# Seven chunks for six in a LoRA projection, with a 16-row store placed between the loads

## The chip, the cores and the metric

The kernel runs on one core of a Trainium2 chip. The metric is the device time of one execution in microseconds (us), lower is better.

## The reference

```python
x_flat = x.reshape(-1, in_dim)              # (16*2048, 256) float32
y = x_flat @ W                              # W: 256 x 256
lora_out = x_flat @ lora_A                  # lora_A: 256 x 16
lora_out = lora_out * lora_E                # 16 values
lora_out = lora_out @ lora_B                # lora_B: 16 x 256
y = y + scale * lora_out
return y.reshape(batch, seq_len, out_dim).astype(np.float32)
```

x and y hold 32,768 rows of 256 float32 each, 33.55 MB in and 33.55 MB out.

## The kernel before

The adapter is folded into the weights first: `weff` = W + A · diag(E · scale) · B, in bfloat16 (lines 148 to 167). After that the kernel is one matrix product, y = x · weff.

**Rows and chunks.** In this text a *row* is a row of one partition: 128 partitions hold one each, so a row of a chunk stands for 128 rows of x, 128 KB. The 256 such rows are cut by `PLAN` into chunks of 48, 32, 48, 48, 48 and 32. A partition's share of a chunk lies contiguously in HBM (`rows_of`), so one transfer of 48 rows moves 48 KB for each of the 128 partitions. `PIECES` lets the loads of chunks 0 and 2 be issued in two pieces each (16 and 32 rows, 24 and 24).

**Slots.** Chunks live in SBUF in four buffers, `SLOTS` = 48, 32, 48 and 48 rows, 176 in all. Chunk i uses slot i modulo 4. The result is written over the input: ScalarE copies y from PSUM into the slot that x came from (line 214), and the store goes out from there. Chunks 4 and 5 use the slots of chunks 0 and 1 again.

**The steps.** A chunk is worked through in steps of S = 8 rows, 32 steps in all. For each step VectorE casts x to bfloat16 (`rounded`, line 141), TensorE transposes it into PSUM as eight blocks (`transposed`, L180), VectorE copies the transposed block to SBUF (`copied`, L145), TensorE multiplies it with `weff` (`multiplied`, L191, 16 matmuls), and ScalarE copies the result into the slot in two halves (L214). VectorE runs two steps ahead in the order copied(t), rounded(t + 2). TensorE runs one step ahead: it transposes step t + 1 before it multiplies step t. So the last step of a chunk is multiplied only after the first step of the next chunk has arrived and been cast.

**The queue of transfers.** All loads and stores of x and y are issued by SyncE, in the order of its program. Before the steps start it issues the first piece of chunk 0, W, the rest of chunk 0, and chunks 1 to 3 (lines 113 to 121). After that, for each chunk in turn, it waits until the chunk's last result has been copied (line 223), issues the store, and then, where `AFTER` names later chunks, waits until the store that frees a slot has landed and issues the load (lines 225 to 227). `AFTER = {1: [4, 5]}` puts loads 4 and 5 behind store 1. The transfers are served in this order: loads 0 to 3, stores 0 and 1, loads 4 and 5, stores 2 to 5.

**The hold.** `HOLD = {3: 1}` makes VectorE wait, ahead of the first cast of chunk 3, until store 1 has landed (lines 136 to 140). The data don't ask for this wait. VectorE works in order, so the copy of the last transposed step of chunk 2, which stands behind it, waits as well, and with it that step's product and store 2.

Of the kernel before, what the change touches and what calls it, by code (L numbers as in the profile page):

```python
# [3 lines left out]

PLAN = [48, 32, 48, 48, 48, 32]

PIECES = {0: [16, 32], 2: [24, 24]}

SLOTS = [48, 32, 48, 48]
LEAD = 4  # L10
AFTER = {1: [4, 5]}

HOLD = {3: 1}

S, G = 8, 4
P = 128
# [17 lines left out]
def kernel(tc, x, W, lora_A, lora_B, lora_E, scale, out):  # L34
    nc = tc.nc
# [5 lines left out]
    KC = K // P  # L41
    assert K == M and sum(PLAN) * P == N
    starts = [sum(PLAN[:i]) * P for i in range(len(PLAN))]

    steps = [(i, r) for i, b in enumerate(PLAN) for r in range(0, b, S)]
    NS = len(steps)
    assert NS % 2 == 0

    def rows_of(flat, i):
        b, r0 = PLAN[i], starts[i]  # L50
        return flat[r0:r0 + b * P, :].rearrange("(p b) k -> p b k", b=b)

    def sbuf(name, shape, dt):
        return nc.alloc_sbuf_tensor(name, shape, dt).ap()
# [3 lines left out]

    slots = [sbuf(f"xy{s}", [P, rows, K], FP32) for s, rows in enumerate(SLOTS)]
    a_sb = sbuf("a_sb", [P, KC, R], FP32)  # L60
# [21 lines left out]
    pieces = {}  # L82
    for i, b in enumerate(PLAN):
        parts = PIECES.get(i, [b])
        pieces[i] = [(sum(parts[:j]), n) for j, n in enumerate(parts)]
    s_ld = {(i, r): Count(nc, f"s_ld{i}_{r}") for i in pieces for r, n in pieces[i]}
    s_st = [Count(nc, f"s_st{i}") for i in range(len(PLAN))]
    s_id, s_set, s_v, s_t, s_m, s_y = (
# [5 lines left out]
    can_y = [[nc.alloc_semaphore(f"can_y{h}_{k}") for k in range(2)] for h in range(S // G)]  # L94

    def slot(i):
        return slots[i % LEAD][:, :PLAN[i], :]

    def load(i, parts=None):
        for r, n in parts or pieces[i]:  # L100
            s_ld[i, r].by(nc.sync.dma_start(out=slot(i)[:, r:r + n, :], in_=rows_of(x_flat, i)[:, r:r + n, :]), 16)

    def store(i):
        s_st[i].by(nc.sync.dma_start(out=rows_of(out_flat, i), in_=slot(i)), 16)
# [6 lines left out]


    with tc.tile_critical(no_gpsimd_drain=True):
        load(0, pieces[0][:1])
        s_w.by(nc.sync.dma_start(out=w_sb, in_=W.rearrange("(p c) m -> p c m", c=KC)), 16)
        s_a.by(nc.scalar.dma_start(out=a_sb, in_=lora_A.rearrange("(p c) r -> p c r", c=KC)), 16)
        s_b.by(nc.scalar.dma_start(out=b_sb, in_=lora_B), 16)
        s_e.by(nc.scalar.dma_start(out=e_sb, in_=lora_E[:, None]), 16)
        load(0, pieces[0][1:])
        for i in range(1, LEAD):  # L120
            load(i)
    tc.close()
    tc.compile()  # L123
# [8 lines left out]
    def rounded(t):  # L132
        i, r = steps[t]
        if (i, r) in s_ld:
            nc.vector.wait_ge(s_ld[i, r].sem, 16)
        if i in HOLD and r == 0:

            for _ in range(10):
                nc.vector.engine_nop()
            nc.vector.wait_ge(s_st[HOLD[i]].sem, 16)  # L140
        nc.vector.tensor_copy(out=xb[t % 2], in_=slot(i)[:, r:r + S, :]).then_inc(can_t[t % 2], 1)  # L141
# [68 lines left out]
    for i, r in [(i, r + g) for i, r in steps for g in range(0, S, G)]:  # L210
        n += 1
        nc.scalar.wait_ge(s_m.sem, n)
        t, h = divmod(n - 1, S // G)
        y = nc.scalar.copy(out=slot(i)[:, r:r + G, :], in_=ps_y[h])  # L214
        free = can_y[h][(t + 1) % 2]
        if r + G < PLAN[i]:
            y.then_inc(free, 1)
        else:
            done = s_y.by(y)
            if n < s_m.total:  # L220
                nc.scalar.wait_ge(s_y.sem, done)
                nc.scalar.sem_inc(free, 1)
            nc.sync.wait_ge(s_y.sem, done)
            store(i)
            for later in AFTER.get(i, []):
                nc.sync.wait_ge(s_st[later - LEAD].sem, 16)
                load(later)


# [44 lines left out]
```

## Time and profile before

| what | value |
|---|---|
| median of 3 runs | 162.41 us (162.36 to 163.22) |
| the profiled execution | 162.57 us |
| its span, first to last recorded instruction | 161.3 us |
| read from HBM, written | 33.85 MB, 33.55 MB |
| mean rate of DMA over the span | 418 GB/s |
| mean granted clock of TensorE | 0.82 |

The profile divides the span into 40 slices and gives, for each engine, the busy share in tenths:

```profile
PE   0149179999999980000009999999999970000000
PEld 0038058999999960000008899999999960000000
DVE  0074197898989800000039589898989500000000
ACT  0300406777768680000000577776868680000000
...
PEclk9999978999999998555555899999999997555555
```

The compute engines work in two blocks, from about 20 to 60 us and from about 84 to 133 us. TensorE's granted clock falls to 0.5 where it stands idle and is back to full some 8 us into a block. The groups by cost show what one instruction of each kind takes (busy time, mean ns, idle time before):

```profile
L214 ACT COPY xy<-psum_y 128x1024 f32<-128x1024 f32 x64 | 61.9, 1015 | 64.0 <-PE psum_y L191 64.0
L191 PE MATMUL psum_y<-weff,xt 128*128 128x256 bf16 x512 | 64.9, 283 | 0.1
L141 DVE CAST xb<-xy 128x2048 bf16<-128x2048 f32 x32 | 39.0, 1217 | 32.3 <-DMA out_dram<-xy 26.8
L145 DVE COPY xt<-psum_xt 128x1024 f32<-128x1024 f32 x32 | 39.2, 1224 | 11.2 <-PE psum_xt L180 11.2
```

The cast's 26.8 us of waiting for a store is the hold.

### The profile page before, as it was taken

To read this page: it belongs to the slowest core of one execution; us is meant where nothing else is said; L and a number is where in the kernel's file an instruction comes from. 1 tells how busy PE (TensorE), PEld (TensorE's weight loads), DVE (VectorE), ACT (ScalarE), POOL (GpSimd) and SP (SyncE) were. 2 spreads that over 40 slices of the span, in tenths; PEclk is the share of its full clock that TensorE was granted. 3 is DMA by queue.
4 is the path that set the end of the run, shared out by engine and by line. 5 is a ranking of instruction groups with operands and counts; after the bars stand their busy time and mean duration, and the time that the engine had idled before them with its cause. 6 is when DMAs were issued, how large, how long until landed. Compare 5 with 4: busy or idle time off the path is not lost.

```text
span 161.3 us, 1875 instructions
## 1 busy us (share of the span) xinstructions
PE 93.2 (58%) x780; PEld 83.4 (52%) x780; DVE 76.6 (48%) x67; ACT 63.2 (39%) x65; POOL 0.7 (0%) x6
## 2 busy tenths in 40 slices
PE   0149179999999980000009999999999970000000
PEld 0038058999999960000008899999999960000000
DVE  0074197898989800000039589898989500000000
ACT  0300406777768680000000577776868680000000
POOL 0100000000000000000000000000000000000000
PEclk9999978999999998555555899999999997555555
DMA  4999999999999999989999989999999999999993
GB/s 137 407 496 423 423 423 433 408 463 408 506 439 427 402 390 392 500 386 398 480 435 402 500 378 406 471 431 404 463 463 415 402 451 463 427 402 402 447 447 171
DMA packets 2370, 67.42 MB, mean 418 GB/s; under 512 B 432, under 2 KB 448, under 8 KB 576
## 3 DMA queue, kind: packets, MB, share of 16 engines
q1 hardware_dynamic: 2160, 67.37, 97.7%
q10 hardware_dynamic: 208, 0.03, 0.1%
q14 instruction: 2, 0.02, 0.0%
HBM read 33.85 MB, written 33.55 MB: 418 GB/s over the span
## 4 chain that ended last, share of the span: by engine, by line
PE 44%; DMA 22%; ACT 2%; DVE 1%; issue 0%
PE psum_y L191 29%; DMA out_dram<-xy 22%; PE psum_xt L180 14%; ACT xy L214 2%; DVE xb L141 1%
## 5 line engine op out<-in xcount | busy, mean ns | idle before, releaser
L214 ACT COPY xy<-psum_y 128x1024 f32<-128x1024 f32 x64 | 61.9, 1015 | 64.0 <-PE psum_y L191 64.0
L191 PE MATMUL psum_y<-weff,xt 128*128 128x256 bf16 x512 | 64.9, 283 | 0.1
L191 PEld LDWEIGHTS psum_y<-weff,xt 128*128 128x128 bf16 x512 | 51.8, 101 | 7.6 <-issue 0.3
L141 DVE CAST xb<-xy 128x2048 bf16<-128x2048 f32 x32 | 39.0, 1217 | 32.3 <-DMA out_dram<-xy 26.8
L180 PE MATMUL psum_xt<-ident,xb 128*128 128x128 f32 x264 | 37.1, 288 | 29.7 <-DVE xb L141 29.7
L180 PEld LDWEIGHTS psum_xt<-ident,xb 128*128 128x128 f32 x264 | 32.3, 150 | 31.3 <-DVE xb L141 30.9
L145 DVE COPY xt<-psum_xt 128x1024 f32<-128x1024 f32 x32 | 39.2, 1224 | 11.2 <-PE psum_xt L180 11.2
L153 PE MATMUL psum_xt<-ident,a_sb 128*16 128x128 f32 x2 | 0.6, 397 | 6.8 <-POOL ident L127 6.8
L149 DVE CAST b_bf<-b_sb 16x256 bf16<-16x256 f32 x1 | 0.3, 281 | 7.9 <-DMA b_sb<-in_lora_B_dram 7.9
L214 ACT ACT_TABLE_LOAD x1 | 1.3, 1283 | 6.0 <-PEq L123 6.0
L153 PEld LDWEIGHTS psum_xt<-ident,a_sb 128*16 128x16 f32 x2 | 0.1, 90 | 6.7 <-DMA a_sb<-in_lora_A_dram 6.7
L162 PE MATMUL psum_xt<-b_bf,ate 16*128 16x256 bf16 x2 | 0.6, 402 | 2.4 <-DVE ate L157 2.4
L162 PEld LDWEIGHTS psum_xt<-b_bf,ate 16*128 16x128 bf16 x2 | 0.1, 104 | 2.9 <-DVE ate L157 2.9
L157 DVE TENSOR_SCALAR ate<-psum_xt,e_sb 16x256 bf16<-16x256 f32 x1 | 0.5, 473 | 1.0 <-DMA e_sb<-in_lora_E_dram 1.0
L167 DVE TENSOR_TENSOR weff<-w_sb,psum_xt 128x512 bf16<-128x512 f32 x1 | 0.7, 669 | 0.0
L127 POOL TENSOR_SCALAR_AFFINE_SELECT ident<-ident 128x128 f32<-128x128 f32 x1 | 0.3, 292 | 0.2 <-POOL ident L125 0.2
L125 POOL MEMSET ident<- 128x128 f32 x1 | 0.2, 205 | 5.4 <-POOLq L123 5.4
L255 POOL MEMSET const-bfloat16-1.0<- 128x1 bf16 x1 | 0.1, 102 | 0.0
L255 POOL MEMSET const-uint8-127<- 128x1 uint8 x1 | 0.1, 101 | 0.0
L255 POOL MEMSET const-float32-0.0<- 128x1 f32 x1 | 0.1, 98 | 0.2 <-issue 0.2
L255 POOL MEMSET const-float32-1.0<- 128x1 f32 x1 | 0.1, 98 | 0.0
## 6 DMA issues: line engine op xcount, KB each, us to landing
out_dram<-xy SPq DMA_DIRECT2D x4, 6144.0 KB, 30.6
xy<-in_x_dram SPq DMA_DIRECT2D x3, 4096.0 KB, 24.5
xy<-in_x_dram SPq DMA_DIRECT2D x2, 6144.0 KB, 39.3
out_dram<-xy SPq DMA_DIRECT2D x2, 4096.0 KB, 31.8
xy<-in_x_dram SPq DMA_DIRECT2D x2, 3072.0 KB, 36.7
xy<-in_x_dram SPq DMA_DIRECT2D x1, 2048.0 KB, 8.4
w_sb<-in_W_dram SPq DMA_DIRECT2D x1, 256.0 KB, 8.5
a_sb<-in_lora_A_dram ACTq DMA_DIRECT2D x1, 16.0 KB, 5.7
```

The lines of the kernel that those rows point to most:

```text
L127: s_id.by(nc.gpsimd.affine_select(out=ident, in_=ident, compare_op=mybir.AluOpType.not_equal, fill=1.0, base=0, pattern=[[-1, P]], channel ...
L141: nc.vector.tensor_copy(out=xb[t % 2], in_=slot(i)[:, r:r + S, :]).then_inc(can_t[t % 2], 1)
L145: nc.vector.tensor_copy(out=xt[t % 2], in_=ps_xt[t % 2]).then_inc(can_m, 1)
L149: s_v.by(nc.vector.tensor_copy(out=b_bf, in_=b_sb))
L153: at_done = nc.tensor.transpose(ps_at[:, c, :], a_sb[:, c, :], ident)
L157: s_v.by(nc.vector.tensor_scalar(out=ate, in0=ps_at, scalar1=e_sb, scalar2=float(scale), op0=mybir.AluOpType.mult, op1=mybir.AluOpType.mult))
L162: aeb_done = nc.tensor.matmul(ps_aeb[:, c, :], ate[:, c, :], b_bf, start=True, stop=True)
L167: s_v.by(nc.vector.tensor_add(out=weff, in0=w_sb, in1=ps_aeb))
L180: done = nc.tensor.transpose(ps_xt[k][:, j, :], words[k][:, j, :], ident)
L191: done = nc.tensor.matmul(ps_y[h][:, j, :], pairs[k][:, h * G + j, :, c], weff[:, c, :], start=(c == 0), stop=(c == KC - 1))
L214: y = nc.scalar.copy(out=slot(i)[:, r:r + G, :], in_=ps_y[h])
L255: nc = _bacc.Bacc("TRN2", target_bir_lowering=False, num_devices=1)
```

## The change

`PLAN` becomes seven chunks of 16, 32, 48, 48, 32, 32 and 48 rows, each loaded in one piece. The slots become five, 16, 32, 48, 48 and 32 rows, again 176 in all. A table `HEIR` replaces the modulo: chunk 5 takes the slot of chunk 1, and chunk 6 that of chunk 2; the slots of chunks 0, 3 and 4 are used once. Only `FIRST` = 3 chunks, 96 rows, are loaded before the first store. `AFTER` puts loads 3 and 4 behind store 0, with no wait for any landing, since their slots have not been used, and loads 5 and 6 behind store 2, which wait for the landings of stores 1 and 2. The hold moves to chunk 4, which waits for store 2. The instructions of TensorE, VectorE, ScalarE and GpSimd are the same, in the same order, but for the place of the hold (step 18 in place of 16) and the waits for loads.

The order of the queue before and after (L load, S store, rows in brackets; W is loaded after the first 16 rows in both):

```
before: L0a(16) W L0b(32) L1(32) L2a(24) L2b(24) L3(48) S0(48) S1(32) L4(48) L5(32) S2(48) S3(48) S4(48) S5(32)
after:  L0(16)  W L1(32)  L2(48) S0(16) L3(48) L4(32) S1(32) S2(48) L5(32) L6(48) S3(48) S4(32) S5(32) S6(48)
```

```diff
-PLAN = [48, 32, 48, 48, 48, 32]
-
-PIECES = {0: [16, 32], 2: [24, 24]}
-
-SLOTS = [48, 32, 48, 48]
-LEAD = 4
-AFTER = {1: [4, 5]}
-
-HOLD = {3: 1}
+PLAN = [16, 32, 48, 48, 32, 32, 48]
+
+PIECES = {}
+
+SLOTS = [16, 32, 48, 48, 32]
+LEAD = 5
+HEIR = {5: 1, 6: 2}
+
+FIRST = 3
+AFTER = {0: [3, 4], 2: [5, 6]}
+
+HOLD = {4: 2}
...
     def slot(i):
-        return slots[i % LEAD][:, :PLAN[i], :]
+        return slots[HEIR.get(i, i)][:, :PLAN[i], :]
...
     with tc.tile_critical(no_gpsimd_drain=True):
-        load(0, pieces[0][:1])
+        load(0)
         s_w.by(nc.sync.dma_start(out=w_sb, in_=W.rearrange("(p c) m -> p c m", c=KC)), 16)
...
-        load(0, pieces[0][1:])
-        for i in range(1, LEAD):
+        for i in range(1, FIRST):
             load(i)
...
             for later in AFTER.get(i, []):
-                nc.sync.wait_ge(s_st[later - LEAD].sem, 16)
+                if later in HEIR:
+                    nc.sync.wait_ge(s_st[HEIR[later]].sem, 16)
                 load(later)
```

## The prediction

> **What bounds the kernel now.** I read the page's busy time first, then the row of DMA shares and the queue table, then the SyncE queue's own waits, and last the timeline around each store's issue.
>
> ```profile
> span 161.3 us, 1875 instructions
> PE 93.2 (58%) x780; PEld 83.4 (52%) x780; DVE 76.6 (48%) x67; ACT 63.2 (39%) x65; POOL 0.7 (0%) x6
> DMA  4999999999999999989999989999999999999993
> q1 hardware_dynamic: 2160, 67.37, 97.7%
> PE psum_y L191 29%; DMA out_dram<-xy 22%; PE psum_xt L180 14%; ACT xy L214 2%; DVE xb L141 1%
> ```
>
> No compute engine is busy for more than 58% of the span. The DMA row reads 9 or 8 in every slice but the first and the last, and one queue's packets fill 97.7% of what 16 engines can do in the span. The chain of waits (last line) names PE, but it follows the last store back through what let it be issued; the queue's own order is not in it. So I checked the SyncE queue's waits (us in total, times, longest), the group of all stores, and the timeline at the last store:
>
> ```profile
> SPq L104 <- ACT xy L214: 90.0, 6, 31.4
> SPq L101 <- DMA out_dram<-xy: 35.0, 2, 25.6
> ...
> DMA to landing us min/median/max: 28.0/30.6/36.5
> ...
> 133.27 0.33 SPq L104 DMA_DIRECT2D out_dram<-xy  x1
> ```
>
> A store takes 28.0 us or more from issue to landing, though its 48 rows need only 14.5 us of transfer (below): it stands behind other transfers. The last store is issued at 133.27 and the span ends at 161.3, with the engines full in between. The path is therefore the first load's start, then one unbroken stream of 67.4 MB. I write L0, L1... for loads, S0, S1... for stores. All go through SyncE's queue, and the landings follow the order of issue.
>
> The trace's records of single packets give the price of the stream. Each transfer puts 8 packets on each of the 16 engines. From one packet's start to the next, undisturbed, it is 1.812 us for 48 rows, 1.209 for 32 and 0.606 for 16: a transfer of 48, 32 or 16 rows holds the engines for 14.50, 9.68 or 4.85 us. The first packet starts at 1.99 us, 1.05 after its issue; the last packet ends at 160.3 and lands at 161.24, 0.95 later. Between these, no engine has a gap. What the packets took over 0.611, 0.912, 1.213 and 1.815 us (16, 24, 32, 48 rows) is 1.57 us per engine: 0.65 at the head, 0.53 from 52 to 64, where loads give way to S0, 0.11 from 104 to 112 (L5 to S2), 0.02 where stores give way to L4 at 82, and about 0.013 to 0.016 per 4 us where compute runs beside the transfers.
>
> ```profile
> 48.00:52.00 4.00, 4.00 (x39) 3.71 (x38) 3.74 (x4) 2.95 (x4) 0.00 (x0) 1.00 1.02 442
> 52.00:56.00 4.00, 4.00 (x39) 3.73 (x38) 3.48 (x4) 2.83 (x3) 0.00 (x0) 1.00 1.11 430
> 56.00:60.00 4.00, 3.68 (x34) 3.14 (x32) 0.57 (x1) 3.09 (x4) 0.00 (x0) 1.00 0.92 393
> 80.00:84.00 4.00, 0.00 (x0) 0.00 (x0) 0.62 (x1) 0.00 (x0) 0.00 (x0) 0.50 1.14 492
> ```
>
> The columns are PE, PEld, DVE, ACT, POOL, clock, DMA share and GB/s. A packet counts where it ends, so one slice swings between 0.9 and 1.14; the turn from loads to stores shows as 430 and then 393 GB/s, the turn back (80 to 84) as no loss.
>
> **The change, part by part.** *Bytes and packets.* Before there are 8 loads and 6 stores, after 7 and 7; 256 rows go in and 256 out in both. 14 transfers of 8 packets per engine stay 14, so the stream's nominal length does not change: 0.
>
> *Is the stream kept unbroken?* The queue becomes L0(16) W L1(32) L2(48) S0(16) L3(48) L4(32) S1(32) S2(48) L5(32) L6(48) S3(48) S4(32) S5(32) S6(48). W ends at about 8.6 in the trace, and up to there the order is unchanged (the 16-row piece of L0 is now L0, the 32-row piece is L1). Adding the prices above, transfers end at: L1 18.3, L2 32.8, S0 37.6, L3 52.1, L4 61.8, S1 71.5, S2 86.0, L5 95.7, L6 110.2, S3 124.7, S4 134.3, S5 144.0, S6 158.5. Each issue must come about 1.05 us before its predecessor's end.
>
> The new danger is S0, since SyncE now waits for chunk 0's results with L3 and L4 behind that wait. Chunk 0 is two steps of 8 rows; PE multiplies step 1 only after it has transposed step 2, which lies in L1. Before, step 2 lay in the 32-row second piece of L0, at the same place of the queue, so the old timeline gives the time: the copies of step 1 are
>
> ```profile
> 23.98 1.01 ACT L214 COPY xy<-psum_y 128x1024 f32<-128x1024 f32 x1 [6.21 <-PE psum_y L191]
> 25.65 1.01 ACT L214 COPY xy<-psum_y 128x1024 f32<-128x1024 f32 x1 [0.66 <-PE psum_y L191]
> ```
>
> so S0 is issued at 25.65 + 1.01 = 26.7, L3 and L4 by 27.9 (0.34 to 0.79 each). The queue would run dry at 32.8: slack 32.8 - 26.7 - 1.05 = 5.0 us. Cost 0.
>
> For the others I take a restart after a pause as 7.7 us from the first cast to the store's issue (83.38 to 91.12 before, at the clock's 0.50) and a step as 2.62 (pairs of ACT copies start at 32.64 and 35.26). L2 lands about 33.8; S1 is issued by 33.8 + 7.7 = 41.5 (needed by 60.7). L3 lands at 53.1, S2 by 60.8 (needed 70.4). L5 waits for S1's landing, 72.5 (needed 84.9); L6 for S2's, 87.0 (needed 94.6, slack 7.6). The hold on chunk 4 (DVE waits for S2; behind it the copy of chunk 3's last step, and with that S3) ends at 87.0: S3 at 94.7 (needed 109.1), S4 four steps later at 105.2 (123.6), S5 after L6's landing at 111.2 + 7.7 = 118.9 (133.3), S6 six steps on, 134.6 (142.9). The least slack is 5.0: nothing of compute, holds or waits reaches the path. Chunk 2 as one load instead of two pieces makes PE pause until 33.8; the 19 us of slack at S1 hide it.
>
> *The turns.* Before the stream turns from loads to stores twice and back once; after, three times and twice. This is the only part on the path. The turn back: 0.02 per engine, taken as 0. The turn to stores: 0.11 and 0.53 per engine in the two rows; seen at the landing of the last engine, L5 comes 9.99 after L4 instead of 9.68 (0.31), and L3 with S0 14.95 + 14.84 instead of 14.55 + 14.50 (0.74). The last engine sets the end, so one more turn costs between 0.31 and 0.74. The dearer row has 48-row packets in all 16 engines' last load slowed to 1.9 to 2.6 us; the cheaper one 32-row packets, of which only some are slowed. The three new ones are 48 to 16 rows, 32 to 32 and 48 to 48. The first resembles the dearer row on its load side, the cheaper in its short store, so I take the middle, 0.5, and keep for the range that it gains (-0.3, if the dear price belongs to the first store ever or to its size) and that all three are dear (3 x 0.74 - 1.05 = +1.2).
>
> The Trainium skill speaks against the change here: its page "DMA: Bandwidth & Descriptors", section "Anatomy of one DMA", gives each DMA about 2 us fixed, mostly the write's receipt (a fit for DMAs that GpSimd issues). If each turn paid that openly, two more turns would be an estimated 4 us. In this queue S3 follows S2 by 14.5 us, its bare transfer, and the turn at 82 shows no gap; the trace disagrees where a successor is already queued.
>
> *The head.* L0's packets now come from rows 16 KB apart per partition instead of 48 KB. The excess there is 0.65; it could go (-0.65) or, by the same size, double. Taken as 0.
>
> Sum: 0 + 0 + 0.5 = +0.5 on the profiled 162.57 (span 161.3 and 1.3 around it), 163.1; the median of the runs is 162.41, 0.16 lower, so the forecast is 162.9.
>
> **The rivals.**
> - *The short store smears its turn* (slower). Engines end 1.4 to 2 us apart, and S0 lasts only 4.85, so some read while others write from L2's end into L3. Price: one slowed 48-row packet of +0.5 (2.3 against 1.8) at L2's end and one or two at L3's start, +0.5 again at the later turns: +1.5 in all, 163.9. It decides when L3's first packets are over 2.0 us. For it: every engine was hit at the old first turn. Against: the turn back at 82 cost nothing.
> - *Turns are cheap or the dear one is only the first*: -0.3, 162.1. For: 0.11 at the second turn. Against: both are the same kind of meeting.
> - *Faster*: the closer rows take the head's 0.65 away and the smaller store takes 0.4 of the first turn (0.53 to 0.11): -1.0, 161.4. Against: from 4 us on L0's packets already run at 0.611.
> - *S0 comes late and starves the queue*: were chunk 0's end to wait for L2, S0 would be issued at 41.5, with the queue dry from 32.8: 41.5 + 1.05 - 32.8 = 9.8, so 172. Against: the two copies above.
> - *Each turn drains the queue*: 1.05 before a first packet and 0.95 after a last are 2.0 per turn, two more turns 4.0, 166.4. (The rule of the Trainium skill above says the same.) Against: no gap at any of three turns.
> - That the store does not stand between the loads I give nothing of its own: landings keep the order of issue.
>
> **How the numbers follow.** Forecast 0.52 (its own range 162.3 to 163.4), smeared turns 0.20, cheap turns 0.10, faster 0.10, starved 0.05, drained 0.03. A measurement of this kernel tells about 0.5%, 0.8 us, from no change: under 161.6 is faster, over 163.2 slower. Faster: 0.10 and 0.02 of the cheap case, 0.12. Slower: 0.28 and 0.06 of the forecast's upper edge, 0.34. The rest, 0.54, is no change. The range 161.8 to 164.2 takes in the smeared and the cheap case and leaves out the starved and drained ones and most of the faster one, 0.18.
>
> **What would show it.** Right: S0 issued near 26.7 and landing near 39; DMA shares at 9 throughout; three dips at about 32, 61 and 109 us; every later store issued long before its turn in the queue; span near 161.8. Wrong: a DMA slice of 7 or less between 30 and 45 (starved); packets of L3 over 2.0 us (smeared); a head whose 16-row packets differ from 0.65 us of excess. A queue share under 96% at a longer span would mean that I missed a gap.

## The result and the profile after

The changed kernel takes 162.75 us in the median of 22 runs (162.53 to 163.28), the kernel before 162.46 us (162.23 to 163.22). The ratio is 1.0019, with a 95% interval of 1.0012 to 1.0026: 0.31 us slower by the ratio (0.19 to 0.42 by its interval), which 22 runs of each can tell from nothing, though it is under the 0.5% set as the bound. The forecast was 162.9 and "no change".

The profiled execution took 163.04 us, the third slowest of the 22 and 0.29 over their median. The lines of the page that answer to those of before:

```profile
span 161.7 us, 1876 instructions
PE 95.8 (59%) x780; PEld 84.4 (52%) x780; DVE 76.0 (47%) x67; ACT 63.2 (39%) x65; POOL 0.7 (0%) x6
DMA  3999999989989999999899999999999999999992
q1 hardware_dynamic: 2160, 67.37, 97.0%
PE psum_y L193 7%; PE psum_xt L182 3%; ACT xy L216 1%
```

The DMA row is still 8 or 9 in every slice but the first and last. The chain of waits (last line) now covers some 11% of the span: it is followed back from the last store, which was issued long before its turn, so it says little of the end in either kernel. The queue of SyncE, first its waits, then the group of all stores, then the timeline at store 0:

```profile
SPq L107 <- ACT xy L216: 98.2, 7, 22.6
SPq L104 <- DMA out_dram<-xy: 28.4, 2, 14.2
...
DMA to landing us min/median/max: 13.1/29.1/31.9
...
26.81 0.35 SPq L107 DMA_DIRECT2D out_dram<-xy  x1
```

Store 0 is issued at 26.81 (26.7 was predicted), and no store waits less than 13.1 us from issue to landing.

So the stream is as unbroken as before, and yet the span is longer. Where the time went shows in the landings. Each transfer ends on 16 DMA engines, and the trace has each engine's landing. The spread between the first and the last engine, in us from the span's start:

```
                     last store: first, median, last engine   spread
kernel before              159.25     159.72     161.22         1.97
changed kernel             159.27     159.51     161.69         2.42
```

The first engine ends at the same time in both kernels, and the median engine even 0.21 us earlier in the changed one. Only the last engine is later. The same spread at each landing from load 1 on (us; L load, S store):

```
kernel before   L1 1.07  L2a 1.06  L2b 1.06  L3 1.15  S0 1.46  S1 1.13  L4 1.46  L5 1.74  S2 1.77  S3 1.97  S4 2.00  S5 1.97
changed kernel  L1 1.04  L2 1.58  S0 1.33  L3 1.52  L4 2.24  S1 2.24  S2 2.08  L5 2.25  L6 2.34  S3 2.37  S4 2.40  S5 2.41  S6 2.42
```

In the changed kernel's trace nearly all of it is there when load 4 lands. Load 2 adds 0.54 us and load 4 adds 0.72; they are the last loads ahead of the first and the second turn from loads to stores, and one packet of load 4 ran over by 729 ns. All that follows adds 0.18. But this is one execution. The changed kernel without its hold (below), the same up to there, has 0.63 and 0.98 us at these two landings, after 0.90 at load 1. Four of the experiments below (the work added behind the last step) are the kernel before up to 133 us, and in these and the kernel before the spread at the landing of load 5 is 1.70 to 2.00 us: one trace of each kernel can't settle 0.3 us.

The excess that I had priced as a mean over the engines fell from 1.57 to 0.99 us, while the time rose: the mean doesn't set the end.

Of that mean, the three turns from loads to stores took 0.32, 0.10 and 0.06 us in the changed kernel, 0.48 in all, against 0.53 and 0.11 before. The head took 0.29 instead of 0.65, but that is one execution: with the same first load it was 0.51, 0.77 and 0.60 in three of the experiments.

Looking for what else makes an engine late, I listed the store packets that took longer than their 1.815 us (48 rows). In the kernel before, from 112 to 132 us, start in us and excess in ns:

```
113.7:90 115.6:113 117.5:99 119.4:109 121.4:112 123.3:99 125.2:99 127.1:109 129.0:123 131.0:109
```

The starts are 1.9 us apart, which is one packet and its excess: these are the successive packets of a single engine, while the 15 others have none over 30 ns. They stop at 132 us, when TensorE stops. A trace doesn't name the engine of a packet; that it is one is read from this spacing. I had read the same numbers as "0.013 to 0.016 per 4 us where compute runs beside the transfers", a mean over 16. On the one engine it is 16 times as much, 0.1 us in 1.8.

The changed kernel has such an engine too. When the packets are joined end to start, it ends 1.87 us behind the first engine in both kernels. Before, that made it the last. In the changed kernel's trace another engine ends last, 2.45 us behind, and none of its store packets ran over. So this trace doesn't show the slowed stores as the cause of the later end.

How much TensorE works beside stores is a view of the profile: the windows in which stores hold the queue (columns PE, PEld, DVE, ACT, POOL, clock, DMA share, GB/s; x is the number of instructions). Before, stores 0 and 1, then 2 to 5:

```profile
57.00:82.00 25.00, 2.68 (x25) 2.23 (x23) 0.00 (x0) 3.07 (x4) 0.00 (x0) 0.62 1.02 439
105.50:160.00 54.50, 26.65 (x245) 24.55 (x242) 20.06 (x17) 20.81 (x22) 0.00 (x0) 0.77 0.98 425
```

After, store 0, then 1 and 2, then 3 to 6:

```profile
33.00:38.00 5.00, 2.20 (x14) 1.90 (x12) 2.89 (x3) 1.68 (x2) 0.00 (x0) 0.77 0.99 423
62.00:86.00 24.00, 9.95 (x92) 8.96 (x89) 6.33 (x6) 8.28 (x9) 0.00 (x0) 0.80 1.01 437
110.50:160.00 49.50, 21.35 (x193) 19.16 (x190) 15.11 (x13) 16.52 (x18) 0.00 (x0) 0.78 0.98 425
```

TensorE is busy beside stores for 29.3 us with 270 matmuls (transposes counted in) before, and for 33.5 us with 299 after. The change puts chunk 3's steps beside store 1 (62 to 71 us).

### The profile page after: what moved, and what is told of

Its sections match the earlier page's. It is cut to its first block, busy times and chain, and to the rows that moved or that the text cites. A ratio compares the mean times of both kernels' runs of the same rounds, so it can differ in the third digit from the quotient of the medians.

```text
span 161.7 us, 1876 instructions
## 1 busy us (share of the span) xinstructions
PE 95.8 (59%) x780; PEld 84.4 (52%) x780; DVE 76.0 (47%) x67; ACT 63.2 (39%) x65; POOL 0.7 (0%) x6
## 5 line engine op out<-in xcount | busy, mean ns | idle before, releaser
L182 PE MATMUL psum_xt<-ident,xb 128*128 128x128 f32 x264 | 38.4, 295 | 27.9 <-DVE xb L143 27.9
L182 PEld LDWEIGHTS psum_xt<-ident,xb 128*128 128x128 f32 x264 | 32.9, 152 | 30.4 <-DVE xb L143 30.0
## 6 DMA issues: line engine op xcount, KB each, us to landing
out_dram<-xy SPq DMA_DIRECT2D x1, 2048.0 KB, 13.1
```

Of the source, the lines that this page charges most:

```text
L182: done = nc.tensor.transpose(ps_xt[k][:, j, :], words[k][:, j, :], ident)
```

## The experiments

The first four runs were made to test the third turn against the chunks, the head and the hold; the one-engine theory came out of them. Ratios are to the kernel before, timed beside it on the same chip. The matmul count is the sum of PE's x over the store windows, as above.

**Two turns.** Loads 3 and 4 go ahead of store 0.

```diff
-FIRST = 3
-AFTER = {0: [3, 4], 2: [5, 6]}
+FIRST = 5
+AFTER = {2: [5, 6]}
```

> The change's chunks and slots, but loads 3 and 4 issued before store 0: the stream turns from loads to stores twice, as in the kernel before, not three times. Theory (the third turn costs the 0.3 us): back to 162.4 to 162.5, ratio 0.999 to 1.001. Rival (the new chunks, the contiguous first load or the place of the hold cost it): 162.75, ratio 1.002. A head that got cheaper (0.29 against 0.65 us of excess per engine in the two traces) would show here alone: 162.1 to 162.3.

Measured: 162.5 us, ratio 1.0001 (0.9985 to 1.0017). Matmuls beside stores: 271. The interval just leaves out 1.0019, so chunks, first load and hold by themselves are hardly the cause, and no gain from the head shows. It speaks for the turn, but the matmul count fell as well.

**The turn alone.** In the kernel before, load 3 goes behind store 0.

```diff
-AFTER = {1: [4, 5]}
+FIRST = 3
+AFTER = {0: [3], 1: [4, 5]}
...
-        for i in range(1, LEAD):
+        for i in range(1, FIRST):
...
-                nc.sync.wait_ge(s_st[later - LEAD].sem, 16)
+                if later >= LEAD:
+                    nc.sync.wait_ge(s_st[later - LEAD].sem, 16)
```

> The kernel before with its own chunks, slots, pieces and hold, but load 3 issued behind store 0: three turns from loads to stores, nothing else changed. Theory: 0.3 us slower than before, 162.7 to 163.0, ratio 1.002 to 1.003, and the last engine's lag behind the first grows at the landing of the load ahead of each turn. Rival (chunks, head, hold): unchanged, 162.46, ratio 1.000.

Measured: 163.62 us, ratio 1.0057 (1.0035 to 1.0079). The direction is the theory's, the size two to three times too large for it. Store 0 now goes out while chunks 1 and 2 are computed:

```profile
42.50:57.50 15.00, 15.00 (x140) 13.98 (x139) 12.38 (x11) 11.30 (x12) 0.00 (x0) 1.00 1.03 442
71.50:81.50 10.00, 0.00 (x0) 0.00 (x0) 0.00 (x0) 0.00 (x0) 0.00 (x0) 0.50 0.99 427
105.50:162.00 56.50, 26.53 (x244) 24.43 (x241) 19.93 (x17) 20.69 (x22) 0.00 (x0) 0.75 0.95 410
```

That is 384 matmuls beside stores. From 42.9 to 56.3 us one engine's packets run 90 to 167 ns over, eight in a row, and the last engine ends 4.1 us behind the first. This profiled execution took 164.62 us, 1.0 over the median, so its spread is not the typical one.

**Four turns.** Load 4 moves behind store 1.

```diff
-AFTER = {0: [3, 4], 2: [5, 6]}
+AFTER = {0: [3], 1: [4], 2: [5, 6]}
```

> The changed kernel with load 4 moved behind store 1: four turns from loads to stores. Theory: another 0.3 us (0.1 to 0.7), 163.0 to 163.3, ratio to the kernel before 1.004 (1.002 to 1.007). Rival (a turn is free once the first is paid): 162.75, ratio 1.002.

Measured: 162.89 us, ratio 1.003 (1.0006 to 1.0054); 279 matmuls beside stores. Between the two expectations it is inconclusive: the interval holds both values. Seven of the twelve executions took 162.31 to 162.96 us, five 163.31 to 163.96.

**No hold.** The changed kernel without its hold.

```diff
-HOLD = {4: 2}
+HOLD = {}
```

> The changed kernel without the hold of chunk 4. Theory (compute is nowhere on the path, packets beside compute take 0.3% longer for the same number of steps): 162.75, ratio 1.002. Rival (the hold keeps compute away from a turn, and its new place costs the time): 0.2 us or more away from 162.75, to either side.

Measured: 163.4 us, ratio 1.0059 (1.0036 to 1.0082), 0.65 us over the changed kernel's median with the same three turns. A premise of my theory fell here: compute does reach the path. Whether a turn costs time as well, this run doesn't tell. Without the hold chunk 4 is computed beside stores 1 and 2; with 28 matmuls beside store 0 it is 410 in all:

```profile
62.00:86.50 24.50, 21.49 (x197) 19.74 (x195) 16.55 (x15) 17.04 (x18) 0.00 (x0) 1.00 1.01 434
110.50:160.00 49.50, 20.52 (x185) 18.35 (x182) 15.11 (x13) 15.70 (x17) 0.00 (x0) 0.75 0.98 424
```

**No hold in the kernel before.** The new theory was put to a kernel with two turns.

```diff
-HOLD = {3: 1}
+HOLD = {}
```

> The kernel before without its hold: still two turns from loads to stores, the same queue, the same chunks, but chunk 3 is computed from about 60 us on, beside stores 0 and 1, and TensorE's work beside stores grows from 28 us to about 41. Theory now (one of the 16 DMA engines serves store packets some 5 to 6% slower while the compute engines work, and that engine ends last; the five runs so far give 0.06 us for each us of compute beside stores): 0.6 to 0.9 us slower, ratio 1.0035 to 1.0055, and one engine with packets 0.05 to 0.12 us longer from about 60 to 77 us. Rival (the number of turns sets the time): ratio 1.000.

Measured: 163.56 us, ratio 1.0061 (1.0041 to 1.0081), with 398 matmuls beside stores. Two turns, and as slow as three turns with 410 matmuls. The direction and the size are the theory's, a little above its range (1.0035 to 1.0055). One engine's packets run 80 to 127 ns over from 61.6 to 71.2 us, as it had said. It also tells what the hold does: it keeps chunk 3's compute away from stores 0 and 1.

```profile
57.00:82.00 25.00, 18.73 (x169) 16.72 (x166) 13.88 (x12) 14.60 (x16) 0.00 (x0) 0.96 1.03 443
105.50:160.00 54.50, 24.99 (x229) 22.96 (x227) 18.66 (x16) 19.27 (x20) 0.00 (x0) 0.77 0.98 425
```

**Which engine does it.** Three kernels add work behind the last step, where in the kernel before no packet is over by more than 21 ns. Its results go to PSUM or SBUF that nobody reads; SyncE starts it with a semaphore once the last result is in.

```diff
...
+    for _ in range(12):
+        for j in range(2 * G):
+            for c in range(KC):
+                nc.tensor.matmul(ps_y[j // G][:, j % G, :], pairs[1][:, j, :, c], weff[:, c, :],
+                                 start=(c == 0), stop=(c == KC - 1))
```

> The kernel before, and behind its last step 192 matmuls more on TensorE alone, into PSUM that nobody reads, from about 134 to 155 us, where stores 4 and 5 go out and no packet was over its time in any of the six traces. If TensorE is what slows the one DMA engine: 8 or more packets of stores 4 and 5 some 0.1 us (48 rows) and 0.07 us (32 rows) longer, about 1 us on the last landing, 163.3 to 163.6. If not: no packet over its time by more than 0.03 us after 135 us, 162.4 to 162.7.

```diff
...
+    for _ in range(18):
+        s_q.by(nc.vector.tensor_copy(out=xt[0], in_=ps_xt[1]))
+        nc.vector.wait_ge(s_q.sem, s_q.total)
...
```

> As before it, with 18 PSUM copies of 128 x 1024 on VectorE alone from about 134 to 157 us. If VectorE slows the one DMA engine: packets of stores 4 and 5 longer by 0.05 to 0.12 us on one engine, 163.3 to 163.6. If not: none, 162.4 to 162.7.

```diff
...
+    for _ in range(20):
+        s_q.by(nc.scalar.copy(out=xt[0], in_=ps_xt[1]))
+        nc.scalar.wait_ge(s_q.sem, s_q.total)
...
```

> As before it, with 20 PSUM copies of 128 x 1024 on ScalarE alone from about 134 to 156 us. If ScalarE slows the one DMA engine: packets of stores 4 and 5 longer by 0.05 to 0.12 us on one engine, 163.3 to 163.6. If not: none, 162.4 to 162.7. If none of the three alone does it, it takes them together or their traffic of semaphores.

The packets that ran over by more than 25 ns from 134 us on (start in us, excess in ns):

```
TensorE:  134.6:90 136.5:98 138.4:80 140.0:412 140.3:71 142.1:85 144.0:80 145.9:71 147.8:80 149.7:99 151.6:60 152.9:61 154.0:369 154.2:47
VectorE:  none
ScalarE:  154.3:33
```

TensorE alone does it, packet after packet until its last matmul starts at 154.5 us. One execution each took 163.54 (TensorE), 162.82 (VectorE) and 163.39 us (ScalarE). The last two miss their expectation of 162.4 to 162.7, but with at most one packet over they do so hardly through the added work. In the run of ScalarE the last engine was 2.6 us behind the first already at store 3, most of which went out before that work began.

**Half the instructions.** The same time on TensorE, with 96 matmuls of 512 columns.

```diff
...
+    wide = weff[:, :, :].rearrange("p c m -> p (c m)")
+    for _ in range(12):
+        for j in range(2 * G):
+            nc.tensor.matmul(ps_y[j // G][:, j % G // 2 * 2:j % G // 2 * 2 + 2, :].rearrange("p g m -> p (g m)"),
+                             pairs[1][:, j, :, 0], wide, start=True, stop=True)
```

> As the run with 192 matmuls of 256 columns behind the last step, but 96 of 512 columns: the same time on TensorE with half the instructions. If the slowing goes with TensorE's busy time: packets of store 4 some 0.1 us longer on one DMA engine, as there. If it goes with the number of its instructions: some 0.05 us. Time 163.3 to 163.6 in the first case, 162.8 to 163.2 in the second.

Measured: 162.85 us, and packets over by 32 to 46 ns, but for one of 80 and a single one of 400, which has its like at 140.0 above:

```
134.6:43 136.4:46 138.3:43 139.6:400 140.1:33 142.0:43 143.8:43 145.7:33 147.5:33 149.4:80 151.3:32
```

The windows of the two kernels, first 256 columns, then 512:

```profile
136.00:152.00 16.00, 16.00 (x149) 14.34 (x148) 0.00 (x0) 0.00 (x0) 0.00 (x0) 1.00 0.99 427
```

```profile
136.00:152.00 16.00, 16.00 (x76) 7.23 (x74) 0.00 (x0) 0.00 (x0) 0.00 (x0) 1.00 0.99 428
```

TensorE is busy for all 16 us in both. Some 8.5 packets at 80 ns are 680 ns over 149 matmuls, 4.6 ns for each; some 8.7 at 41 ns are 357 ns over 76, 4.7 ns. The slowing goes with the number of TensorE's instructions, not with its busy time. The weight loads halve along with the matmuls (PEld 14.34 and 7.23 us), so which of the two counts isn't told. These are single executions.

**Finer pieces.** Two kernels lower the count by starting TensorE earlier. In the kernel before:

```diff
-PIECES = {0: [16, 32], 2: [24, 24]}
+PIECES = {0: [16, 16, 16], 1: [16, 16], 2: [24, 24], 3: [16, 32]}
...
-        if i in HOLD and r == 0:
+        if i in HOLD and r == 16:
```

> The kernel before with chunks 0, 1 and 3 loaded in finer pieces (16, 16, 16; 16, 16; 16, 32) and the hold moved to row 16 of chunk 3, so that TensorE starts about 5 us earlier and does two steps more beside the first loads. Same queue, two turns. Theory (TensorE beside stores costs 0.06 us per us): that overlap falls from 28 to about 22 us, -0.4 us, and 4 more loads (4 x 8 packets x 0.006 us) cost 0.2: ratio 0.997 to 0.999. Rival (the number of transfers or turns sets the time): ratio 1.001 or more.

> The finer pieces in the kernel before once more, since 0.9992 with an interval of 0.997 to 1.0015 told nothing: theory 0.998 to 0.9995, rival 1.001 or more.

Measured: 162.55 us, ratio 0.9992 (0.997 to 1.0015), and once more 162.61 us, 0.9992 (0.9973 to 1.001). The counts are 228 and 226. The first lies just above its expectation (0.997 to 0.999), the second inside its own, and neither interval leaves out 1: it is not shown to be faster than the kernel before.

In the changed kernel:

```diff
-PIECES = {}
+PIECES = {1: [16, 16], 2: [24, 24], 3: [24, 24]}
```

> The changed kernel with chunks 1, 2 and 3 loaded in two pieces each (16, 16; 24, 24; 24, 24): the same queue and the same three turns, but TensorE waits less for whole loads and is nearly through chunk 3 when store 1 goes out. Matmuls beside stores should fall from 295 to about 240, under the 265 of the kernel before. If TensorE beside stores is what the change cost: ratio to the kernel before 0.999 to 1.001, in spite of three turns and three more loads. If the third turn is what it cost: 1.002 to 1.003.

Measured: 162.61 us beside 162.62 of the kernel before, ratio 0.999 (0.9973 to 1.0008). The queue has the same order, three turns and three more loads, and the loss is gone. That rules out a fixed price of 0.2% or more for a third turn. It does not decide on the turn: the pieces lower the count and, at the same time, make the packets of load 2 ahead of the first turn half as long (24 rows for 48). The spread is 0.56 us there, after 0.60 at load 1, where the changed kernel's trace went from 1.04 to 1.58. The count is 269, not the 240 I expected, but that of the kernel before:

```profile
33.00:38.00 5.00, 5.00 (x49) 4.66 (x47) 4.40 (x5) 3.62 (x5) 0.00 (x0) 1.00 1.01 431
62.00:86.50 24.50, 3.56 (x33) 3.03 (x31) 0.46 (x1) 3.85 (x4) 0.00 (x0) 0.66 1.00 431
110.50:160.00 49.50, 20.74 (x187) 18.55 (x185) 15.11 (x13) 15.91 (x17) 0.00 (x0) 0.78 0.98 424
```

All kernels with repeated runs, in order of the count:

| kernel | turns to stores | matmuls beside stores | ratio |
|---|---|---|---|
| before, finer pieces (again) | 2 | 226 | 0.9992 |
| before, finer pieces | 2 | 228 | 0.9992 |
| changed, finer pieces | 3 | 269 | 0.9990 |
| before | 2 | 270 | 1 |
| changed, two turns | 2 | 271 | 1.0001 |
| changed, four turns | 4 | 279 | 1.0030 |
| changed | 3 | 299 | 1.0019 |
| before, turn alone | 3 | 384 | 1.0057 |
| before, no hold | 2 | 398 | 1.0061 |
| changed, no hold | 3 | 410 | 1.0059 |

From 270 up to some 400 matmuls the time follows the count, with two turns as with three. Below 300 the table orders nothing by itself. The kernel with four turns is out of the order of the count: 9 matmuls more than before, at 7 ns each (below), make 1.0004, under its interval of 1.0006 to 1.0054. And the three kernels with the changed chunks, the hold and whole loads come in the order of their turns: 1.0001, 1.0019 and 1.0030 for two, three and four.

## Why the prediction was right in its number and wrong in a step

*What bounds it* was right: the stream of transfers, with the compute engines free. *The unbroken stream* was right: store 0 was issued at 26.81 for 26.7 and the last store at 134.61 for 134.6. In between SyncE was up to 2.1 us late (load 5 at 74.56 for 72.5, load 6 at 89.05 for 87.0), within the slack, and no slice of the DMA row but the first and the last is below 8. The starved and faster rivals are out. So is the drained one: on the first engine store 3 lands 14.48 us after load 6, its bare transfer. The Trainium skill's page "DMA: Bandwidth & Descriptors" (section "Anatomy of one DMA") gives each DMA that GpSimd issues about 2 us fixed. At a turn of this full queue, which SyncE issues, the trace shows none of it.

*The turns*, the only term of the sum, are neither confirmed nor refuted. I took 0.5 us for one turn more from the last engine's landings before. For it speak the landings of loads 2 and 4 in the changed kernel's trace and the order of the kernels with whole loads. Against it, the same landings without the hold show no such growth, the turns' mean cost did not grow, and the kernel with three turns and finer pieces has no loss. A price for every turn is excluded by that run; a price for a turn behind 48-row packets is not. The first packets of load 3 ran at 1.815 us, so the short store smears nothing there.

The step that failed is "nothing of compute, holds or waits reaches the path", and under it "about 0.013 to 0.016 per 4 us where compute runs beside the transfers". The runs without a hold show it: in the kernel before it cost 0.6% that compute moved beside stores 0 and 1 (1.0061), and the work added behind the last step says that of the three engines it is TensorE. The cost was in the table and I priced it as a mean over 16 engines. Beside stores it sits on one, and the end is that of the slowest.

How much of the 0.31 us comes from this step is not shown. 29 matmuls more at 4.6 ns are 0.13 us; in the kernel's own steps it is nearer 5.7 ns (106 ns over some 19 matmuls in a packet's time, at 39 in 4 us), which makes 0.17. By the slope of the table (128 to 140 matmuls more for 0.96 to 0.99 us, some 7 ns each) they are 0.2, at the lower end of the measured 0.19 to 0.42. In the one trace of the changed kernel the slowed engine isn't the last. So the cause of the 0.31 us stays open between the turns and TensorE's work beside stores. A kernel with three turns, whole loads and the count of the kernel before would tell; it was not tried. Part of the gap between these prices and 7 ns may be that an engine that lags is still loading when the others turn to stores and is slowed again there: in the run with the turn alone one packet at 105.0 us ran 938 ns over. That was not tried by itself either.

*The place of the hold* was costed at nothing, by slack in the queue. The slack is real, but the hold is worth 0.4% in the changed kernel and 0.6% in the one before, since it keeps TensorE away from stores.

*The head* at 0 was as good as any guess: its mean excess differs from execution to execution by more than between the kernels.

That the number came out near (0.5 us predicted, 0.31 measured) is in part luck. The term is the middle of two readings, 0.31 and 0.74, of one execution, and the spread at load 5 differs by 0.3 us between executions of the same instructions. One execution could not tell a turn's price from that scatter. "No change" rests on the unbroken stream and on a bound of 0.8 us, and that was right.

## What to carry to other kernels

Where a stream of transfers fills the queue, look at the spread of the landings over the DMA engines, not at the mean share: one engine that is 5% slow for 30 us can move the end and leaves the mean at 97%. In such a kernel, place dense TensorE work beside loads rather than beside stores, which was worth up to 0.6% here, and count what an edit of the queue's order does to that overlap as well as to the turns. A difference of 0.2% between two kernels is not explained by one trace of each. A wait that the data don't ask for may be there to do just this.

## What the runs showed of the hardware

Store packets of one of the 16 DMA engines took about 0.1 us longer per 1.815 us while TensorE ran the kernel's steps. With work on TensorE alone it was 4.6 to 4.7 ns for each matmul with its weight load, and VectorE or ScalarE alone did nothing of the kind in one execution each. Packets of loads beside the same work were over by 5 ns or so on every engine (1.820 for 1.815). Why TensorE's instructions slow one engine's stores, whether it is always the same engine, and whether an execution without the profiler has it, stays open.
